# Differential attention with the transposed weights as the stationary operand, and 72-wide transposes of the maxima

## The chip, the cores and the metric

The program runs on one core of a Trainium2 chip. The metric is the time of one execution on the device in microseconds (us). Engines are named as in the profile: PE is TensorE (the matmuls; PEld its loads of the stationary operand), DVE VectorE, ACT ScalarE, POOL GpSimd, SP the engine that issues most DMAs.

## The reference

Two layers of a transformer-like block over 128 context rows and 512 latent rows of width 1024. Each layer projects the rows, runs three groups of heads beside each other, projects back and ends in a gated MLP. The change lies in the two attention groups. Shortened:

```python
def gqa_attend(q, k, v):            # 8 heads of 64, 2 key/value heads
    s = einsum('bqkgd,bskd->bkgqs', q, k) * 64 ** -0.5
    p = softmax(s, axis=-1)
    return einsum('bkgqs,bskd->bqkgd', p, v)

def diff_attend(q, k, v, lam):      # 4 heads, two softmaxes of 32-wide keys each
    s = einsum('bqhcd,bshcd->bhcqs', q, k) * 32 ** -0.5
    p = softmax(s, axis=-1)
    a = p[:, :, 0] - lam * p[:, :, 1]
    return einsum('bhqs,bshd->bqhd', a, v)     # v is 64 wide

o_d = rms_norm(diff_attend(...), diff_subln_g) * (1 - lam_init)
```

Latent rows attend to 512 latent and 128 context keys (640), context rows to the 128 context keys alone.

## The kernel before

Everything is float32; products that need the accuracy of float32 are split into high and low float32r parts, and some are plain float32 matmuls. Rows come in five tiles of 128 (t = 0 the context, 1 to 4 latent). In the attention stage of a layer (`attend`, line 1545, called for tiles 1, 2, 3, 4, 0, numbered i) one tile does the following.

- GQA half: `scores` with queries as stationary operand into PSUM pairs `p`; `maxima` on VectorE; `split_m` (1596) puts a group's four negated maxima and their low parts in an [128, 8] tile `mm`; `m_trans` (1604) turns it by a matmul with the identity, 8 wide, into partitions 64 to 72 of a bank, from where it goes to rows 64 to 72 of `qTm`. Those rows meet rows 64 to 72 of `KL`, which are ones, so that the second score matmul (`c_mm`, keys stationary, 512 columns) comes out with the maximum subtracted. `c_exp` takes the exponential on ScalarE into the weight buffers `whi` and `wlo` (PT slots), `d_mm` (1656) multiplies the values `VG` (64 wide, stationary) with it: two matmuls of 512 columns, one for each half of the array's columns, for each of five key blocks. They gather in bank b3, which `o_read` copies out.
- Row sums: for i < 3 `sum_mm` (1690) multiplies 32 ones with the summed exponentials into 64 rows, `sum_c` copies them, `sum_t` (1701) transposes them in four pieces, `sum_r` takes the reciprocal. For i = 3 and 4 eight matmuls of one column (1675) do it.
- Differential half: scores, exponentials `P` with their row sums, the two softmaxes joined, then for each key block four transposes of `P` (`trans`), a copy to a PT slot, and `d_mm` (1794): four matmuls with `VD` (64 wide) as stationary and 128 columns of transposed weights, in pairs in the two halves of the array's columns. They also gather in bank b3 (`od_b`). `o_read2` (1806) copies it, `n_trans` (1816) turns it back with two transposes, `n_copy` and `n_sq` (1823, 1827) read that bank, and the norm, a last turn and a copy into `mix` follow.
- Keys, in the stage before: `split3` (1302) makes high and low parts of the keys, `k_trans` (1315) transposes them, the GQA keys' low part 64 wide.

Two schedulers set the order. `Schedule` (573) orders the tasks of a layer's attention by priority and by free banks (b3 alone for both halves' results, b0 to b2 for the rest). Then `Graph` (181) plans the whole program fifteen times with durations from `cost` (501), each time with new due times, and emits the order with the shortest planned total; it may split what one task emitted. Each engine then runs its instructions in that order. A float32 matmul's planned duration depends on its stationary width (64 wide: half) and its columns.

## Time and profile before

| | us |
|---|---|
| median of three runs (1703.84 to 1709.37) | 1704.2 |
| the profiled execution | 1706.38 |
| its span, first to last instruction | 1704.3 |
| PE busy | 1674.7 (98%) |
| DVE busy | 1027.5 (60%) |
| ACT busy | 680.7 (40%) |
| POOL busy | 215.0 (13%) |
| granted clock of PE, mean | 0.997 of full speed |

The busy times are unions: matmuls overlap, since one starts to stream while the one before still drains, and the profile models their ends. So the cost of a matmul is read from its start to the start of the next. The names in the rows are those of tiles: `b`, `c` and `p` are PSUM banks, "b<-wlo,VG 128*64 128x512" is a matmul with the stationary operand VG of 128 by 64 and the moving operand wlo with 512 columns. "x4" merges four records that follow each other. One matmul in plain float32 leaves two records.

### The profile page before, as it was taken

To read this page: it belongs to the slowest core of one execution; us is meant where nothing else is said; L and a number is where in the kernel's file an instruction comes from. 1 tells how busy PE (TensorE), PEld (TensorE's weight loads), DVE (VectorE), ACT (ScalarE), POOL (GpSimd) and SP (SyncE) were. 2 spreads that over 40 slices of the span, in tenths; PEclk is the share of its full clock that TensorE was granted. 3 is DMA by queue.
4 is the path that set the end of the run, shared out by engine and by line. 5 is a ranking of instruction groups with operands and counts; after the bars stand their busy time and mean duration, and the time that the engine had idled before them with its cause. 6 is when DMAs were issued, how large, how long until landed. Compare 5 with 4: busy or idle time off the path is not lost.

```text
span 1704.3 us, 24487 instructions
## 1 busy us (share of the span) xinstructions
PE 1674.7 (98%) x9771; PEld 1411.9 (83%) x9771; DVE 1027.5 (60%) x1691; ACT 680.7 (40%) x1268; POOL 215.0 (13%) x308
## 2 busy tenths in 40 slices
PE   7999999999999999999999999999999999999998
PEld 4678766678999879999778896657799998999986
DVE  4757677547665768687446568785666543444423
ACT  6453577536322112232255527774633321223310
POOL 1321234201000000000032112351100000000000
PEclk9999999999999999999999999999999999999999
DMA  9543100253333544454334211003233322222221
GB/s 329 176 147 112 37 13 13 64 172 93 112 110 98 179 142 144 134 169 135 101 127 115 69 50 41 22 3 109 74 99 111 109 85 80 83 73 72 75 70 76
DMA packets 156542, 171.53 MB, mean 101 GB/s; under 512 B 6556, under 2 KB 121612, under 8 KB 155916
## 3 DMA queue, kind: packets, MB, share of 16 engines
q1 hardware_dynamic: 150940, 152.18, 29.0%
q0 software_dynamic: 5488, 17.79, 3.2%
q8 instruction: 77, 1.26, 0.3%
q14 instruction: 37, 0.30, 0.1%
HBM read 163.88 MB, written 6.06 MB: 100 GB/s over the span
## 4 chain that ended last, share of the span: by engine, by line
PE 92%; DVE 3%; ACT 3%; DMA 1%; issue 1%; POOL 0%; ACTq 0%; DVEq 0%; POOLq 0%
PE c L316 48%; PE b L316 41%; PE p L316 3%; DVE xq L316 1%; DVE sq L316 1%; ACT whi L316 1%; ACT xn L316 1%; DVE wlo L316 1%; ACT fu L316 0%; DMA raw<-in_w_mod_dram 0%; ACT junk L316 0%; DVE qsg L316 0%; DVE nmax L316 0%; DVE macc L316 0%; ACT hh L316 0%
## 5 line engine op out<-in xcount | busy, mean ns | idle before, releaser
L316 DVE TENSOR_TENSOR wlo<-raw,whi 128x1024 fp32r<-128x1024 f32 (+1 forms) x188 | 227.3, 1209 | 331.3 <-ACT whi L316 331.0
L316 PE MATMUL c<-hl,whi 128*128 128x322 f32 x1280 | 397.9, 311 | 1.1 <-DVE hl L316 1.1
L316 PE MATMUL c<-hh,whi 128*128 128x322 f32 x1280 | 398.5, 312 | 0.0
L316 ACT ACTIVATE whi<-raw 128x1024 fp32r<-128x1024 f32 (+1 forms) x188 | 195.3, 1041 | 506.9 <-PE b L316 283.6
L316 PE MATMUL c<-hh,wlo 128*128 128x322 f32 x1280 | 397.3, 311 | 0.0
L316 PEld LDWEIGHTS c<-hh,whi 128*128 128x128 f32 x1280 | 241.5, 189 | 2.6 <-issue 2.1
L316 PEld LDWEIGHTS c<-hl,whi 128*128 128x128 f32 x1280 | 241.2, 188 | 1.4 <-DVE hl L316 1.3
L316 PEld LDWEIGHTS c<-hh,wlo 128*128 128x128 f32 x1280 | 241.3, 189 | 0.0
L316 DVE SCALAR_TENSOR_TENSOR macc<-raw,slc,macc 128x1024 f32<-128x1024 f32 x98 | 123.8, 1279 | 16.6 <-DMA raw<-in_w_mod_dram 16.2
L316 DVE TENSOR_REDUCE nmax<-p 128x1 f32<-128x640 f32 x128 | 103.7, 819 | 34.3 <-PE p L316 33.8
L316 PE MATMUL b<-wlo,fh 128*128 128x512 f32 x264 | 104.3, 395 | 0.0
L316 PE MATMUL b<-whi,fh 128*128 128x512 f32 x264 | 104.2, 395 | 0.0
L316 PE MATMUL b<-whi,fl 128*128 128x512 f32 x264 | 104.1, 394 | 0.0
L316 PE MATMUL b<-hh,wlo 128*128 128x322 f32 x320 | 99.7, 311 | 0.0
L316 PE MATMUL b<-hh,whi 128*128 128x322 f32 x320 | 99.5, 311 | 0.0
L316 PE MATMUL b<-hl,whi 128*128 128x322 f32 x320 | 99.5, 311 | 0.0
L316 ACT ACTIVATE tv<-tv 128x644 f32<-128x644 f32 x44 | 32.6, 742 | 140.3 <-DVE tv L316 140.2
L316 DVE SCALAR_TENSOR_TENSOR tv<-asb,vec,tv 128x643 f32<-128x643 f32 x88 | 78.0, 887 | 2.3
L316 DVE TENSOR_TENSOR tv<-tv,c 128x322 f32<-128x322 f32 x88 | 42.5, 488 | 53.1 <-ACT tv L316 27.5
L316 PE MATMUL c<-whi,fh 128*128 128x512 f32 x176 | 69.6, 397 | 0.6 <-DVE tv L316 0.6
L316 PE MATMUL c<-wlo,fh 128*128 128x512 f32 x176 | 69.5, 395 | 0.0
L316 PE MATMUL c<-whi,fl 128*128 128x512 f32 x176 | 69.3, 394 | 0.0
(318 smaller groups left out, 3129.5 us busy)
## 6 DMA issues: line engine op xcount, KB each, us to landing
raw<-in_w_mod_dram SPq DMA_DIRECT2D x96, 512.0 KB, 4.0
raw<-in_ffn_up_dram SPq DMA_DIRECT2D x88, 512.0 KB, 4.7
raw<-in_ffn_down_dram SPq DMA_DIRECT2D x40, 512.0 KB, 3.7
raw<-in_w_in_dram SPq DMA_DIRECT2D x28, 512.0 KB, 4.8
raw<-in_w_in_dram SPq DMA_DIRECT2D x16, 256.0 KB, 5.1
raw<-in_w_out_dram SPq DMA_DIRECT2D x8, 512.0 KB, 3.5
raw<-in_w_out_dram SPq DMA_DIRECT2D x16, 256.0 KB, 3.9
gate<-gd POOLq DMA_DIRECT2D x4, 1024.0 KB, 6.0
```

The costliest lines, as they stand in the source:

```text
L316: getattr(real, name)(*a, **k)
```

## The change

- `d_mm` of the differential half swaps its operands: the transposed weights (128 wide) are stationary, 64 columns of `VD` move, and the output has queries on the partitions. The four heads lie side by side in b3. `o_read2` and `n_trans` go; `n_copy` and `n_sq` read `od_b` itself, so b3 is held until both are done.
- `mm` is one of four fixed tiles of [128, 72] whose first 64 columns are cleared by GpSimd at the start of the stage; `m_trans` is 72 wide and writes partitions 0 to 72. What follows reads 64 to 72 as before.
- The low part of the GQA keys is put first in its stack, and its transpose is 72 wide, of which 64 rows are used.
- `sum_mm` multiplies 64 ones instead of 32, the copy and the transposes are 128 by 128.
- `cost` plans a plain float32 matmul with a stationary operand over 64 wide at 4/2400 us for each column or 0.112 us, whichever is more. Since planned durations and tasks change, so does the order.

```diff
+        if m > 64:
+            return max(4 * n / 2400, 0.112), 0.0
...
-            tt(s[:, :, lo_, :], z, f32(s)[:, :, 0, :], ALU.subtract)
+            tt(s[:, :, lo_, :], z, f32(s)[:, :, hi.start, :], ALU.subtract)
...
-                kst["g", t] = split3(T(prj, [128, 2, 3, 64], "kstg", F32R, bufs=1), zv("kg", t), 2, 64, slice(0, 2))
+                kst["g", t] = split3(T(prj, [128, 2, 3, 64], "kstg", F32R, bufs=1), zv("kg", t), 2, 64, slice(1, 3))
...
-                    PE.transpose(pv[:, u, :], v[:, u, 0:128], ident)
-                    PE.transpose(pv[0:64, 2 + u, :], v[:, u, 128:192], ident)
+                    PE.transpose(pv[:, u, :], v[:, u, 64:192], ident)
+                    PE.transpose(pv[0:72, 2 + u, :], v[:, u, 0:72], ident)
...
+        mx_tiles = [T(at, [128, 72], f"mm{x}") for x in range(4)]
+        for x in mx_tiles:
+            G.memset(x[:, 0:64], 0.0)
...
-                def split_m(mm=mm, nm_=nm_):
-                    mm["t"] = T(SM, [128, 8], "mm", bufs=6)
-                    V.tensor_copy(mm["t"][:, 0:4].bitcast(F32R), nm_["t"])
-                    tt(mm["t"][:, 4:8], nm_["t"], mm["t"][:, 0:4], ALU.subtract)
+                def split_m(mm=mm, nm_=nm_, x=mx_tiles[(2 * i + a_) % len(mx_tiles)]):
+                    mm["t"] = x
+                    V.tensor_copy(x[:, 64:68].bitcast(F32R), nm_["t"])
+                    tt(x[:, 68:72], nm_["t"], x[:, 64:68], ALU.subtract)
...
-                    PE.matmul(bk.t[64:72, 0:128], mm["t"], ident, start=True, stop=True)
+                    PE.matmul(bk.t[0:72, 0:128], mm["t"], ident, start=True, stop=True)
...
-                        PE.matmul(sb.t[32 * a_:32 * a_ + 32, :], ones[:, 0:32], x[a_].t, start=True, stop=True)
+                        PE.matmul(sb.t[64 * a_:64 * a_ + 64, :], ones[:, 0:64], x[a_].t, start=True, stop=True)
...
-                        PE.transpose(sb2.t[:, 64 * u:64 * u + 64], box["s"][:, 128 * u:128 * u + 128], ident[0:64, 0:64])
+                        PE.transpose(sb2.t[:, 128 * u:128 * u + 128], box["s"][:, 128 * u:128 * u + 128], ident)
...
-            od_b = Buf(o_bank, 1)
+            od_b = Buf(o_bank, 2)
...
-                    for x in range(2):
-                        for a_ in range(2):
-                            h = 2 * x + a_
-                            PE.matmul(od_b.t[64 * a_:64 * a_ + 64, 128 * x:128 * x + 128], VD[:, v, 64 * h:64 * h + 64],
-                                      pt.t[:, 128 * h:128 * h + 128], start=k == 0 and x == 0, stop=k == len(vs) - 1 and x == 1)
+                    for h in range(4):
+                        PE.matmul(od_b.t[:, 64 * h:64 * h + 64], pt.t[:, 128 * h:128 * h + 128], VD[:, v, 64 * h:64 * h + 64],
+                                  start=k == 0 and h == 0, stop=k == len(vs) - 1 and h == 3)
...
-            def o_read2():
-                oc2.t = T(at, [128, 512], oc2.tag)
-                act(oc2.t[:, 0:256], od_b.t[:, 0:256])
...
-                two(tb.t, oc2.t)
...
-                act(od.t, heads(tb.t[:, 0:256], 64))
+                act(od.t, heads(od_b.t[:, 0:256], 64))
...
-                act(bx["sq"], heads(tb.t[:, 0:256], 64), AF.Square)
+                act(bx["sq"], heads(od_b.t[:, 0:256], 64), AF.Square)
```

How the order moves, at three places of the first layer. The numbers behind a name tell one tile from the next of the same name, `ident` is the identity of a transpose, `qsd` and `qsg` are query stacks. The first place is on PE in the GQA half of the second tile, where value products (VG) stand among scores. Before the change PE has there:

```order
L316 MATMUL p_503_2544<-KL_814,qTm_437_2274 128x320
L316 MATMUL b_483_2485<-whi_2158,VG_842 64x512
L316 MATMUL b_504_2554<-qTg_310_2018,KG_1259 128x512
L316 MATMUL b_504_2554<-qTm_311_854,KL_814 128x512
L316 MATMUL b_506_2563<-ident_109,qsd_2291 96x128 x4
L316 MATMUL b_483_2485<-whi_2158,VG_842 64x512
L316 MATMUL p_509_2571<-KG_1259,qTg_436_2276 128x320
```

Two value products stand there, each alone between full-width matmuls. After the change, at the same place on PE:

```order
L316 MATMUL p_508_2579<-KL_807,qTm_439_2223 128x320
L316 MATMUL b_509_2585<-ident_109,qsd_2306 96x128 x4
L316 MATMUL b_491_2515<-whi_2127,VG_839 64x512
L316 MATMUL b_491_2515<-wlo_2181,VG_839 64x512
L316 MATMUL b_511_2597<-qTg_310_2022,KG_1259 128x512
```

Two value products that stood alone, with scores and transposes between them, stand side by side. In the same tile three stand in a row, twice.

The second place is on PE where the differential half of that tile starts its value products: sums, `mm` and `VD`. Before the change:

```order
L316 MATMUL b_533_2691<-whi_2102,VD_867 64x128 x3
L316 MATMUL b_534_2697<-ident_109,sums_2687 128x64 x4
L316 MATMUL b_533_2691<-whi_2102,VD_867 64x128
L316 MATMUL b_536_2705<-ident_109,P_466_2417 128x128
L316 MATMUL b_536_2705<-ident_109,P_474_2451 128x128
L316 MATMUL b_536_2705<-ident_109,P_484_2487 128x128
L316 MATMUL b_536_2705<-ident_109,P_502_2531 128x128
L316 MATMUL p_539_2718<-KD_939,qTd_429_2246 128x320 x2
L316 MATMUL b_541_2721<-ident_109,mm_2707 8x128
L316 MATMUL b_533_2691<-whi_2102,VD_867 64x128 x2
L316 MATMUL b_542_2730<-ident_109,rx_2716 128x128 x4
L316 MATMUL b_533_2691<-whi_2102,VD_867 64x128 x2
```

The first `d_mm` is cut in two by the sums' transposes (three matmuls and one), the second by the spread of the reciprocals (`rx`), with `mm` beside it. After the change, on PE from the sums' transposes on:

```order
L316 MATMUL b_530_2693<-ident_109,sums_2683 128x128 x4
L316 MATMUL b_532_2701<-VD_865,whi_2107 128x64 x4
L316 MATMUL b_533_2706<-ident_109,P_466_2422 128x128
L316 MATMUL b_533_2706<-ident_109,P_474_2456 128x128
L316 MATMUL b_533_2706<-ident_109,P_484_2492 128x128
L316 MATMUL b_533_2706<-ident_109,P_499_2530 128x128
L316 MATMUL p_536_2717<-KD_946,qTd_431_2259 128x320 x2
L316 MATMUL b_537_2720<-ident_109,mm_368_2030 72x128
L316 MATMUL b_532_2701<-VD_865,wlo_2113 128x64
L316 MATMUL b_538_2726<-ident_109,rx_2713 128x128 x4
L316 MATMUL b_532_2701<-VD_865,wlo_2113 128x64 x3
```

The first `d_mm` is in one piece now; the second is still cut by `rx`, and `mm` still stands beside a part of it, with 128 and 72 columns of the array instead of 64 and 8.

The third place is on ACT at the end of the first tile's differential half: the reads of its result. Before the change:

```order
L316 ACTIVATE ob_479_2467<-b_452_2353 128x256
L316 ACTIVATE wlo_2107<-b_475_2463 128x512
L316 ACTIVATE P_482_2478,sum_2418<-p_472_2454,nmax_2393 128x640
L316 ACTIVATE P_484_2487,sum_2418<-p_476_2469,nmax_2475 128x640
L316 ACTIVATE osq_2497<-b_487_2491 128x256
L316 ACTIVATE whi_2102<-b_477_2473 128x512
L316 ACTIVATE od_489_2509<-b_487_2491 128x256
```

The copy `ob` alone reads the bank of the value products there (b_452); `osq` and `od` read another bank, after the turn. After the change, on ACT from the first read on:

```order
L316 ACTIVATE od_479_2479<-b_453_2357 128x256
L316 ACTIVATE P_482_2486,sum_2423<-p_472_2458,nmax_2388 128x640
L316 ACTIVATE P_484_2492,sum_2423<-p_476_2472,nmax_2477 128x640
L316 ACTIVATE whi_2107<-b_477_2475 128x512
L316 ACTIVATE osq_2505<-b_453_2357 128x256
```

The copy `ob` is gone, `od` and `osq` read the bank of the value products itself (b_453), and two exponentials and a copy stand between them; that bank is b3, which the next tile's GQA half needs.

## Rows read from the trace of the kernel before

**Rows 1.** The page, chain that ended last: its time by engine, whole span.

```profile
PE 92%; DVE 3%; ACT 3%; DMA 1%; issue 1%; POOL 0%; ACTq 0%; DVEq 0%; POOLq 0%
```

**Rows 2.** Busy us of each engine (instructions), clock, DMA: the two attention stages.

```profile
196.00:345.00 149.00, 148.36 (x832) 90.69 (x831) 107.23 (x197) 102.36 (x232) 54.39 (x62) 0.98 0.14 42
1036.00:1183.00 147.00, 146.39 (x830) 92.14 (x831) 110.25 (x198) 103.55 (x233) 54.95 (x62) 1.00 0.12 40
```

**Rows 3.** TensorE's instructions in time: start us, us, what; full-width neighbours.

```profile
209.15 0.40 PE L316 MATMUL b<-qTg,KG 128*128 128x512 f32 x1
209.38 0.39 PE L316 MATMUL b<-qTm,KL 72*128 72x512 f32 x1
```

**Rows 4.** The same view: transposes, then the one-column sums.

```profile
309.48 0.66 PE L316 MATMUL b<-ident,P 128*128 128x128 f32 x4
309.97 1.84 PE L316 MATMUL b<-ones,acc 128*128 128x1 f32 x16
311.67 0.63 PE L316 MATMUL b<-ident,P 128*128 128x128 f32 x4
```

**Rows 5.** The same view: a whole d_mm, and a half one.

```profile
228.24 0.40 PE L316 MATMUL b<-qTm,KL 72*128 72x512 f32 x1
228.56 0.66 PE L316 MATMUL b<-whi,VD 128*64 128x128 f32 x8
229.15 0.50 PE L316 MATMUL b<-qTg,KG 128*128 128x512 f32 x1
229.49 0.39 PE L316 MATMUL b<-qTm,KL 72*128 72x512 f32 x1
...
318.63 0.44 PE L316 MATMUL b<-wlo,VD 128*64 128x128 f32 x4
319.00 0.66 PE L316 MATMUL b<-KD,qTd 96*128 96x128 f32 x4
```

**Rows 6.** The same view: a pair of VG, and a single one.

```profile
207.13 1.08 PE L316 MATMUL b<-whi,VG 128*64 128x512 f32 x4
208.14 0.42 PE L316 MATMUL p<-KD,qTd 96*128 96x320 f32 x1
...
214.82 0.31 PE L316 MATMUL p<-KG,qTg 128*128 128x320 f32 x1
214.97 0.31 PE L316 MATMUL p<-KL,qTm 72*128 72x320 f32 x1
215.21 1.07 PE L316 MATMUL b<-wlo,VG 128*64 128x512 f32 x2
216.22 0.42 PE L316 MATMUL p<-KG,qTg 128*128 128x320 f32 x1
```

**Rows 7.** The same view: transposed maxima, and the transposes of the sums.

```profile
218.71 0.31 PE L316 MATMUL p<-KG,qTg 128*128 128x320 f32 x1
218.95 0.39 PE L316 MATMUL b<-ident,mm 128*8 128x128 f32 x2
219.26 0.42 PE L316 MATMUL p<-KL,qTm 72*128 72x320 f32 x1
...
223.16 0.46 PE L316 MATMUL b<-ident,sums 64*128 64x64 f32 x4
223.55 0.56 PE L316 MATMUL p<-KD,xq 96*128 96x320 f32 x2
```

**Rows 8.** Weight loads by shape: count, busy us, mean ns of one, idle.

```profile
L316 PEld LDWEIGHTS b<-ones,acc 128*128 128x128 f32 x32 | 3.7, 192 | 0.0
```

**Rows 9.** ScalarE by shape: exponentials, copy of 512 columns, squares of 256.

```profile
L316 ACT ACTIVATE P<-p,nmax 128x640 f32<-128x640 f32 x64 | 50.8, 796 | 9.4 <-DVE nmax L316 8.1
...
L316 ACT ACTIVATE ob<-b 128x512 f32<-128x512 f32 x10 | 5.9, 593 | 4.9 <-PE b L316 4.8
...
L316 ACT ACTIVATE osq<-b 128x256 f32<-128x256 f32 x10 | 3.8, 382 | 2.8 <-PE b L316 2.8
```

**Rows 10.** As rows 2: the stretch in which the clock fell.

```profile
321.30:328.20 6.90, 6.90 (x18) 3.04 (x17) 1.93 (x10) 2.51 (x8) 1.82 (x5) 0.51 0.31 77
```

More of the change, by code (lines that the diff above doesn't have):

```diff
@@ L1692, in sum_mm @@
                     for a_ in range(2):
-                        PE.matmul(sb.t[32 * a_:32 * a_ + 32, :], ones[:, 0:32], x[a_].t, start=True, stop=True)
+                        PE.matmul(sb.t[64 * a_:64 * a_ + 64, :], ones[:, 0:64], x[a_].t, start=True, stop=True)
                 s1 = sc.add([("PE", 0.5, sum_mm)], aT, p_, takes=[sb], reads=accs)
                 def sum_c(e, sb=sb, box=box):
-                    box["s"] = T(at, [64, 512], "sums")
-                    act(box["s"], sb.t[0:64]) if e is S else e.tensor_copy(box["s"], sb.t[0:64])
+                    box["s"] = T(at, [128, 512], "sums")
+                    act(box["s"], sb.t) if e is S else e.tensor_copy(box["s"], sb.t)
                 s1 = sc.add([("S", 0.48, lambda f=sum_c: f(S)), ("V", 0.6, lambda f=sum_c: f(V))], [s1], p_, reads=[sb])
@@ L1796, in d_mm @@
                         od_b.t = bank(od_b.tag)
-                    for x in range(2):
-                        for a_ in range(2):
-                            h = 2 * x + a_
-                            PE.matmul(od_b.t[64 * a_:64 * a_ + 64, 128 * x:128 * x + 128], VD[:, v, 64 * h:64 * h + 64],
-                                      pt.t[:, 128 * h:128 * h + 128], start=k == 0 and x == 0, stop=k == len(vs) - 1 and x == 1)
+                    for h in range(4):
+                        PE.matmul(od_b.t[:, 64 * h:64 * h + 64], pt.t[:, 128 * h:128 * h + 128], VD[:, v, 64 * h:64 * h + 64],
+                                  start=k == 0 and h == 0, stop=k == len(vs) - 1 and h == 3)
                 d_prev = sc.add([("PE", 0.48, d_mm)], [e_, d_prev], p_ + 2, takes=[od_b] if k == 0 else [], reads=[pt])
             p_ = base + P_TD + I_T * (3 + len(vs))
-            oc2 = Buf(s_ob, 1)
-            def o_read2():
-                oc2.t = T(at, [128, 512], oc2.tag)
-                act(oc2.t[:, 0:256], od_b.t[:, 0:256])
-            n1 = sc.add([("S", 0.27, o_read2)], [d_prev], p_, takes=[oc2], reads=[od_b])
-            tb = Buf(banks, 2)
             def two(dst, src):
@@ L1814, in two @@
                     PE.transpose(dst[:, 128 * x:128 * x + 128], src[:, 128 * x:128 * x + 128], ident)
-            def n_trans():
-                tb.t = bank(tb.tag)
-                two(tb.t, oc2.t)
-            n2_ = sc.add([("PE", 0.22, n_trans)], [n1], p_, takes=[tb], reads=[oc2])
             od = Buf(s_od, 1)
@@ L1824, in n_copy @@
                 od.t = T(at, [128, 4, 64], od.tag)
-                act(od.t, heads(tb.t[:, 0:256], 64))
+                act(od.t, heads(od_b.t[:, 0:256], 64))
             def n_sq():
                 bx["sq"] = T(at, [128, 4, 64], "osq")
-                act(bx["sq"], heads(tb.t[:, 0:256], 64), AF.Square)
-            n3 = sc.add([("S", 0.27, n_copy)], [n2_], p_, takes=[od], reads=[tb])
-            n4 = sc.add([("S", 0.27, n_sq)], [n2_, n3], p_, reads=[tb])
+                act(bx["sq"], heads(od_b.t[:, 0:256], 64), AF.Square)
+            n3 = sc.add([("S", 0.27, n_copy)], [d_prev], p_, takes=[od], reads=[od_b])
+            n4 = sc.add([("S", 0.27, n_sq)], [d_prev, n3], p_, reads=[od_b])
             def n_sum():
```

2 lines of the change are left out of this document (1 added, 1 removed).

## The prediction, made before the result was known

> **What bounds the kernel now.** I read the chain that ended last first, then the busy time of the two attention stages, then TensorE's instructions one by one. The chain runs over TensorE for 92% of the span [rows 1]. The two attention stages last 149 and 147 us; TensorE is busy for all but 0.6 us of each, VectorE for 107 and 110 us, ScalarE for 102 and 104 [rows 2]. So in the stages that the change touches nothing but TensorE's own instruction stream sets the time, and the question is what each of its instructions costs there. A "busy" TensorE is not one that streams, so I price by the distance from one start to the next, not by the printed durations (they overlap).
>
> **The plain prices.** Beside other full-width matmuls one of 320 columns takes 0.15 us to the next start and one of 512 columns 0.23 [rows 3, 6]. Four transposes right behind a narrow piece take 0.49, so at most 0.12 each with the way out of that piece in it; I take 0.11. Eight one-column matmuls show as 16 records, so a plain float32 matmul leaves two; the 16 take 1.70, 0.106 each [rows 4].
>
> **What a narrow matmul costs.** I call narrow what uses 64 or fewer columns or rows of the array. Take one d_mm of the differential half: the 512-column matmul ahead of it lasts 0.32 to the next start instead of 0.23, its eight records take 0.59, and the 512-column matmul behind it lasts 0.34 instead of 0.23 [rows 5]. So each trip into the narrow form and out again puts some 0.09 and 0.11, together 0.20, on its full-width neighbours, and one d_mm is worth 0.79. Broken into two halves, as the order often has it, a half takes 0.37 itself and the like of 0.10 at either side: 0.57 [rows 5]. Two pairs more make 0.22, so a pair streams in 0.11, and 0.59 less four pairs leaves 0.15 inside for filling and emptying. A value product of the GQA half (VG) takes 0.24 - 0.15 ahead, 1.01 itself, some 0.10 behind: 1.20. Two of them side by side also take 1.01 [rows 6], so the second is free if the order leaves it beside the first. The transposed maxima (mm, 8 wide) cost 0.09 + 0.31 and some 0.10 behind, 0.50; the four transposes of the row sums (64 by 64) take 0.39 themselves, 0.58 with both sides [rows 7].
>
> **The change part by part, both layers together.** Counts are from the program's order.
>
> *VG* itself is unchanged but stands otherwise: before in 61 pieces (38 single, 23 pairs), after in 48 (24 single, 14 pairs, 8 threes, 2 fours). Before 61 x 1.20 = 73.2. After 38 x 1.20 + 10 x 2.06 = 66.2; the 2.06 is a piece with a second pair, 0.86 more, which is 1.01 less the 0.15 for filling and emptying. Gain 7.0.
>
> *The differential d_mm*, 42 of them. Before: 42 x 0.79 = 33.2, and since they stand in 54 pieces, 12 times a second half at 2 x 0.57 - 0.79 = 0.35, 4.2 more: 37.4. After: the transposed weights are the stationary side, 128 wide, and 64 value columns stream. No row of before shows a float32 matmul of that shape. Nearest is the one-column matmul with the same stationary width, 0.106 a record [rows 4]; 128-column transposes at 0.11 lie on the other side of 64 columns, so I take 0.11: 42 x 8 x 0.11 = 37.0. The bounds are 0.05 (half the 0.11 that a 128-column pair took) and 0.19, the mean duration of a weight load of that width, if no load were hidden [rows 8]. Gain 0.4, between 20 and -26.
>
> The Trainium skill speaks against this swap: "TensorEngine Tiling (Array Packing)", Performance Considerations, wants a matmul with a small streamed side turned so that the small side is stationary and two run side by side in column tiles. That is the form of before; what the swap costs by this rule alone is rival 4. The same page, Key Properties, says that a change of tiling mode drains TensorE; the 0.20 at d_mm's neighbours and the 0.15 inside agree with that and, 42 x 0.35 = 14.7 and the 4.2 of broken pieces, weigh as much as the doubled streaming.
>
> *Maxima 72 wide*: 20 x 0.50 = 10.0 before; after two full-width records of 128 columns, 20 x 0.22 = 4.4. Gain 5.6. *Sums*: 6 groups of four transposes, 6 x 0.58 = 3.5 before, 24 x 0.11 = 2.6 after. Gain 0.9. The sum matmuls keep two pieces side by side and their 512 columns: nothing. ScalarE's copy of the sums has the same 512 columns in a row: nothing.
>
> *Shared borders*: 26 of before's narrow pieces touch another narrow one (mm beside VD, sums inside VD), so 26 x 0.20 = 5.2 of the prices above were never paid. Loss 5.2.
>
> *The removed turn* (o_read2, n_trans): 20 transposes on TensorE, 20 x 0.11 = 2.2 gained, and ten ScalarE copies of 0.38 (the shape of osq [rows 9]), hidden before as well.
>
> *The new hold on bank b3*: n_copy and n_sq now read od_b itself, and the next tile's first VG needs that bank. In tiles 1 and 2 of both layers ScalarE does od, two exponentials and an eviction before osq: about 0.38 + 2 x 0.80 + 0.59 + 0.38 = 2.95 [rows 9]. TensorE has 6 x 0.15 + 8 x 0.23 = 2.7 of other work meanwhile. A wait of 0.25 four times, 1.0 lost; between 0 and 4 x 1.
>
> *Keys' low rows 72 wide* and the halves of the key split in another order: the same number of transposes; a transpose keeps its 128 streamed columns and its 0.11. Nothing. *Eight small memsets* on GpSimd, before the first maxima: GpSimd is busy for 54 of 149 us [rows 2]. Nothing. *The planner's new prices* move instructions in the first 25 us and in the attention; elsewhere the order is the same but for names.
>
> **Sum.** -7.0 - 0.4 - 5.6 - 0.9 + 5.2 - 2.2 + 1.0 = -9.9. The profiled execution took 1706.4 us (its span 1704.3 and 2.1 around it), 2.2 above the median of 1704.2. So 1696.5 for such an execution, and 1694.3 against the median; the start, ordered anew, may give or take 1. I say 1694.5.
>
> **The rivals.**
> 1. *The freed time turns into waits.* With TensorE 5 us shorter per layer, maxima on VectorE or exponentials on ScalarE end last in places, bank b3 above all. For: ScalarE and VectorE are busy for some 70% of these stages [rows 2]. Against: TensorE waited next to nothing there. If half is lost: 1699.5.
> 2. *The clock.* At the end of the first layer's attention the granted clock was 0.51 over 6.9 us, that is TensorE mostly at 1.2 instead of 2.4 GHz, after one-column matmuls, transposes and VD; in the second layer the same stretch ran at 1.00 [rows 2, 10]. After the change this stretch streams no more than before: eight transposes, the one-column matmuls and VD at 64 columns stand there together. If both layers fall, or an earlier place does, each time costs about 3 us (half of 6.9): 1697.5 to 1700.5. If the present one goes, 3 less: 1691.5.
> 3. *Slower: the loads of the new stationary side show.* Each of the 336 records brings 128 columns of weights in and streams only 64. If loads were not hidden, a record would last 0.19, not 0.11: 336 x 0.08 = 27 more, 1721. It turns to a loss where a record lasts over 0.11 + 9.9/336 = 0.14. Against it: the one-column records have loads of 0.19 as well and still follow each other at 0.106 [rows 4, 8].
> 4. *Slower: pairs side by side are what counts.* If d_mm's neighbours stay as slow as they are and its 0.15 inside stays too, for whatever reason, only the streaming changes, from four pairs to eight records: 42 x (0.88 - 0.44) = 18.5 lost instead of 0.4 gained, 1713. Against it: a 512-column matmul without a narrow neighbour takes 0.23, every time one of them has it 0.32 to 0.34 [rows 3, 5]. This is where the Trainium skill's rule on small streamed sides, named above, would end.
> 5. *More than that*: the shorter chain at the end of each attention (one ScalarE copy, one pair of transposes) or a clock that stays up: 1690.
>
> **How the numbers follow.** The forecast has 0.68, its own range 1690 to 1699. Rival 1 has 0.13, rival 2 0.09, rival 3 0.04, rival 4 0.02, rival 5 0.04. About 0.3%, 5.1 us, is what a measurement of this kernel can tell from no change. Range 1689 to 1702. Faster by more than 0.3% (under 1699.1) is the forecast, rival 5 and a part of rival 2: 0.75. Within 0.3%: rival 1, the rest of 2, some of the forecast: 0.19. Slower: rivals 3 and 4: 0.06.
>
> **What would show it.** In the profile after: d_mm's eight records 0.88 from the first start to the next, and a 0.23 behind and ahead of them, not 0.32 and 0.34; mm 0.22; sums 0.44; VG pieces at 1.2 and 2.1, fewer of them; both attention stages some 4 to 5 us shorter with TensorE still busy throughout; no idle TensorE ahead of the first VG of a tile, or 0.25. Wrong would be records at 0.15 or more, TensorE waiting for osq by 1 us, or stages as long as before with waits in them. The rest of the program should take the same time.

## The result, and the profile after

The kernel after the change takes 1722.4 us (median of 5 runs, 1719.2 to 1728.8), the kernel before beside it 1707.4 (1703.8 to 1710.7): a ratio of 1.0095, 95% interval 1.0065 to 1.0124. That is 15 us slower where 10 us less were forecast. The runs of after had a mean granted clock of 0.985 to 0.991 (median 0.989), those of before 0.993 to 0.999 over the whole record (median 0.997). The medians and ratios here and below leave out three runs, one each of before, e6 and e11, that took at least a fifth longer than all others.

The profiled execution of after, the slowest of its five, took 1728.8 us, 22.4 more than that of before. By landmarks on TensorE (the first GQA score, then the first matmul with `mah`, which ends the attention stage), the start took 3.4 us more, the first attention stage 11.7, the second 7.1, and all the rest 0.2. The windows of [rows 2] lie some 10 us later than these landmarks. The two stages in whole, by the view of busy time by window (window, length, then busy us and instructions of PE, PEld, DVE, ACT, POOL, then the granted clock), first of before:

```profile
185.70:338.10 152.40, 151.32 (x866) 93.98 (x864) 111.27 (x206) 106.29 (x243) 54.20 (x62) 0.98 0.10 29
1025.40:1173.10 147.70, 146.11 (x852) 92.50 (x850) 112.25 (x207) 107.58 (x244) 55.06 (x63) 1.00 0.09 29
```

and of after:

```profile
189.10:353.20 164.10, 157.84 (x857) 112.59 (x856) 114.14 (x208) 103.29 (x236) 56.15 (x68) 0.92 0.08 24
1040.70:1195.50 154.80, 147.82 (x840) 103.97 (x838) 113.93 (x208) 104.40 (x237) 55.63 (x67) 0.97 0.08 27
```

Length less PE busy is the time in which TensorE had nothing to do: 1.1 and 1.6 us before, 6.3 and 7.0 after. And the clock fell, from 0.98 and 1.00 to 0.92 and 0.97: 37.5 us of the two stages ran at half clock (0.50, which is 1.2 GHz) instead of 6.8, and about half of such time is lost (sixteen records of VD take 3.3 us in it, eight 0.81 outside). So the 18.8 us that the stages lost in this execution are 10.6 of idle time and 15.3 of clock, while the rest, what TensorE's own work takes at full clock, became 7.1 shorter. The chain that ended last, which ran over VectorE for 3% [rows 1], now does so for 7%:

```profile
PE 89%; DVE 7%; ACT 2%; POOL 1%; DMA 1%; issue 1%; SPq 0%; POOLq 0%; ACTq 0%; DVEq 0%
```

TensorE's waits in the first stage of after (what waits, for what: us in total, times, longest); before, none of them was longer than 0.4 us:

```profile
PE p L316 <- ACT P L316: 2.4, 3, 2.0
PE b L316 <- DVE od L316: 1.3, 1, 1.3
PE b L316 <- ACT qTm L316: 0.9, 2, 0.6
PE p L316 <- DVE nmax L316: 0.8, 3, 0.3
PE b L316 <- DVE mm L316: 0.8, 1, 0.8
```

The prices, on the other hand, are those forecast. One d_mm of after, from TensorE's instructions in time (start us, us, what), beside [rows 5]:

```profile
263.18 0.40 PE L316 MATMUL b<-qTm,KL 72*128 72x512 f32 x1
263.41 1.00 PE L316 MATMUL b<-VD,whi 128*128 128x64 f32 x8
264.22 0.47 PE L316 MATMUL b<-qTg,KG 128*128 128x512 f32 x1
264.54 0.39 PE L316 MATMUL b<-qTm,KL 72*128 72x512 f32 x1
```

0.23 to the first record, 0.81 for the eight, 0.32 for the matmul behind them: 0.90 with what the neighbours lose, 0.88 forecast.

Where the waits are made is seen on VectorE. In the middle of the first stage (after; VectorE's and GpSimd's instructions in time, then TensorE's; the bracket is the idle time ahead and what ended it):

```profile
266.00 0.88 DVE L316 SCALAR_TENSOR_TENSOR P<-P,ra,P 128x640 f32<-128x640 f32 x1
...
267.95 0.22 DVE L316 SCALAR_TENSOR_TENSOR ra<-ra,nl,sum 128x1 f32<-128x1 f32 x1
...
272.73 1.79 DVE L316 SCALAR_TENSOR_TENSOR P<-P,ra,P 128x640 f32<-128x640 f32 x1
274.44 1.51 DVE L316 TENSOR_TENSOR od<-od,ors 128x256 f32<-128x256 f32 x1
...
275.99 1.37 DVE L316 TENSOR_TENSOR od<-od,sg 128x256 f32<-128x256 f32 x1
277.29 0.81 DVE L316 TENSOR_REDUCE nmax<-p 128x1 f32<-128x640 f32 x1
...
272.57 3.10 POOL L316 TENSOR_TENSOR acc<-acc,wlo 128x512 f32<-128x512 f32 x2
275.63 4.08 POOL L316 TENSOR_TENSOR acc<-acc,whi 128x512 f32<-128x512 f32 x3
...
275.84 0.31 PE L316 MATMUL p<-KL,qTm 72*128 72x320 f32 x1
277.42 0.44 PE L316 MATMUL b<-ident,od 128*128 128x128 f32 x2 [1.26 <-DVE od L316]
278.15 0.41 PE L316 MATMUL p<-KG,qTg 128*128 128x320 f32 x1 [0.29 <-DVE nmax L316]
```

While GpSimd adds up exponentials (`acc`, five adds in a row), VectorE's P<-P,ra,P takes 1.79 instead of 0.88, and the two steps of the norm 1.51 and 1.37 instead of 0.42; the reduction nmax, which reads PSUM, keeps its 0.81. TensorE stands for 1.26 us until `od` is there, and again for the maximum that queued behind it. Some 28 us later the same is seen, ahead of the longest wait of the stage:

```profile
300.87 1.66 DVE L316 SCALAR_TENSOR_TENSOR P<-P,ra,P 128x640 f32<-128x640 f32 x1
...
302.64 1.27 DVE L316 SCALAR_TENSOR_TENSOR ra<-ra,nl,sum 128x1 f32<-128x1 f32 x1
303.95 1.85 DVE L316 SCALAR_TENSOR_TENSOR P<-P,ra,P 128x640 f32<-128x640 f32 x1
...
300.57 1.28 POOL L316 TENSOR_TENSOR acc<-whi,wlo 128x512 f32<-128x512 f32 x1 [14.53 <-ACT wlo L316]
302.61 1.29 POOL L316 TENSOR_TENSOR acc<-whi 128x512 f32<-128x512 f32 x1 [0.76 <-ACT whi L316]
303.86 1.26 POOL L316 TENSOR_TENSOR acc<-acc,wlo 128x512 f32<-128x512 f32 x1
...
307.51 0.56 PE L316 MATMUL p<-KD,xq 96*128 96x320 f32 x2 [1.96 <-ACT P L316]
```

The one-column step ra<-ra,nl,sum takes 1.27 instead of 0.22. The exponential of P for which TensorE waits had itself waited 2.5 us for a maximum that stood behind these three. The stretches of both stages at half clock (windows as above):

```profile
278.80:282.20 3.40, 3.40 (x11) 1.36 (x10) 2.02 (x3) 0.59 (x1) 0.92 (x1) 0.50 0.00 0
309.60:313.00 3.40, 3.40 (x5) 0.79 (x4) 3.40 (x9) 1.48 (x3) 1.92 (x2) 0.51 0.00 0
323.20:343.70 20.50, 20.50 (x86) 17.90 (x84) 6.48 (x21) 8.11 (x25) 1.89 (x5) 0.50 0.01 2
1057.10:1063.90 6.80, 6.60 (x10) 2.30 (x11) 3.16 (x7) 3.76 (x10) 1.25 (x1) 0.50 0.28 99
1162.90:1166.30 3.40, 3.40 (x5) 0.79 (x4) 3.40 (x9) 1.48 (x3) 1.97 (x2) 0.50 0.00 0
```

The first two begin 1.4 and 2.1 us after the end of the two waits shown, and the last in the same way after a wait of 1.97 us in the second stage; the fourth stands among waits of 0.6 to 0.7 us. One wait of 1.26 us in the second stage has no fall behind it. The long stretch, 20.5 us, has no wait ahead of it: transposes, one-column matmuls, `mm` and VD stand there, and TensorE is busy throughout. Before, the clock fell for 6.9 us at the end of the first stage [rows 10] and not in the second.

The collisions are not new. Groups of VectorE's instructions by shape over both stages (count, busy us, mean ns of one), before:

```profile
L316 DVE TENSOR_TENSOR od<-od,ors 128x256 f32<-128x256 f32 x10 | 7.9, 793 | 3.8 <-POOL ors L316 3.6
L316 DVE TENSOR_TENSOR od<-od,sg 128x256 f32<-128x256 f32 x10 | 5.3, 534 | 0.1
```

and after:

```profile
L316 DVE TENSOR_REDUCE nmax<-p 128x1 f32<-128x640 f32 x128 | 103.2, 817 | 43.0 <-PE p L316 42.7
...
L316 DVE TENSOR_TENSOR od<-od,ors 128x256 f32<-128x256 f32 x10 | 9.5, 947 | 2.9 <-POOL ors L316 2.8
L316 DVE TENSOR_TENSOR od<-od,sg 128x256 f32<-128x256 f32 x10 | 9.0, 902 | 0.1
```

They got worse for `od`, but a good part of them was there before. What is new is that TensorE waits for them. The Trainium skill describes such a collision ("SBUF — State Buffer", Who interferes with whom): a VectorE instruction with two inputs in SBUF contends with a GpSimd instruction that reads SBUF, and a reduction never contends. The rows above agree, with 0.42 against 1.37 to 1.51 and an unchanged 0.82.

### The profile page after: what moved, and what is told of

It is laid out like the page before. It is cut to its first block, busy times and chain, and to the rows that moved or that the text cites. A ratio compares the mean times of both kernels' runs of the same rounds, so it can differ in the third digit from the quotient of the medians.

```text
span 1727.0 us, 24436 instructions
## 1 busy us (share of the span) xinstructions
PE 1687.1 (98%) x9751; PEld 1446.4 (84%) x9751; DVE 1033.3 (60%) x1693; ACT 675.1 (39%) x1254; POOL 221.1 (13%) x318
## 3 DMA queue, kind: packets, MB, share of 16 engines
q8 instruction: 77, 1.26, 0.3%
## 4 chain that ended last, share of the span: by engine, by line
PE 89%; DVE 7%; ACT 2%; POOL 1%; DMA 1%; issue 1%; SPq 0%; POOLq 0%; ACTq 0%; DVEq 0%
PE c L316 48%; PE b L316 38%; PE p L316 2%; DVE nmax L316 2%; DVE wlo L316 1%; DVE P L316 1%; DVE xq L316 1%; DVE od L316 1%; DMA raw<-in_w_mod_dram 1%; ACT whi L316 0%; DVE sq L316 0%; ACT fu L316 0%; POOL acc L316 0%; ACT xn L316 0%; DVE qsg L316 0%
## 5 line engine op out<-in xcount | busy, mean ns | idle before, releaser
L316 DVE SCALAR_TENSOR_TENSOR macc<-raw,slc,macc 128x1024 f32<-128x1024 f32 x98 | 123.9, 1279 | 13.2 <-DMA raw<-in_w_mod_dram 12.8
```

Of the source, the lines that this page charges most:

```text
L316: getattr(real, name)(*a, **k)
```

## The experiments

Three theories stood against each other at first. **A**: the clock falls because the swapped d_mm streams 64 columns. **B**: the order is at fault, planned with prices that are too low, so that others come late. **E**, after the first four runs: the order lays VectorE's collisions with GpSimd on TensorE's path. All runs in one table; idle is a stage's length less its PE busy, the clock that of the stage, and the last column the part of the stage in which the trace has the clock at 0.50, each from the profiled execution, first stage and second. Length less idle time less half of the last column is called the stream: what TensorE's own work takes at full clock. Both stages together it is 294.0 us before and 286.9 after.

| | median us | ratio to before, 95% | stages us | idle us | clock | at half clock, us |
|---|---|---|---|---|---|---|
| before | 1707.4 | | 152.4, 147.7 | 1.1, 1.6 | 0.98, 1.00 | 6.8, 0.0 |
| after | 1722.4 | 1.0065 to 1.0124 | 164.1, 154.8 | 6.3, 7.0 | 0.92, 0.97 | 27.3, 10.2 |
| e1 | 1717.6 | 1.0037 to 1.0081 | 155.2, 155.7 | 6.3, 7.0 | 0.98, 0.97 | 6.8, 10.2 |
| e2 | 1708.2 | 1.0001 to 1.0032 | 151.2, 149.0 | 3.0, 3.4 | 0.98, 0.99 | 6.8, 3.4 |
| e3 | 1698.6 | 0.9934 to 0.9972 | 145.3, 143.7 | 2.5, 1.7 | 0.98, 0.98 | 6.8, 6.8 |
| e4 | 1725.1 | 1.0088 to 1.0143 | 160.6, 157.1 | 5.5, 6.7 | 0.95, 0.97 | 17.1, 10.2 |
| e5 | 1697.1 | 0.9930 to 0.9955 | 144.2, 145.3 | 2.0, 2.6 | 0.98, 0.98 | 6.8, 6.8 |
| e6 | 1709.6 | 1.0000 to 1.0028 | 154.1, 149.6 | 8.1, 7.4 | 0.94, 0.97 | 17.1, 10.2 |
| e7 | 1702.4 | 0.9965 to 0.9990 | 155.1, 144.3 | 1.8, 2.9 | 0.93, 1.00 | 20.5, 0.0 |
| e8 | 1702.4 | 0.9964 to 0.9985 | 150.1, 148.6 | 1.3, 1.7 | 0.98, 0.99 | 6.8, 3.4 |
| e9 | 1707.3 | 0.9988 to 1.0010 | 154.0, 149.2 | 1.0, 1.6 | 0.97, 0.99 | 10.2, 3.4 |
| e10 | 1701.0 | 0.9960 to 0.9991 | 154.1, 143.7 | 1.1, 1.8 | 0.93, 1.00 | 20.5, 0.0 |
| e11 | 1692.9 | 0.9905 to 0.9931 | 143.4, 142.5 | 1.1, 1.8 | 0.98, 0.99 | 6.8, 3.4 |
| e12 | 1700.4 | 0.9956 to 0.9982 | 146.3, 145.0 | 1.8, 2.8 | 1.00, 1.00 | 0.0, 0.0 |
| e13 | 1702.3 | 0.9954 to 0.9976 | 148.8, 146.0 | 1.8, 2.8 | 0.98, 0.99 | 6.8, 3.4 |
| e14 | 1703.2 | 0.9966 to 0.9991 | 148.3, 148.4 | 1.5, 2.1 | 0.99, 0.99 | 3.4, 3.4 |

**e1, VD streamed 128 wide, same order.**

```diff
-PE.matmul(od_b.t[:, 64 * h:64 * h + 64], pt.t[:, 128 * h:128 * h + 128], VD[:, v, 64 * h:64 * h + 64],
+PE.matmul(od_b.t[:, 128 * h:128 * h + 128], pt.t[:, 128 * h:128 * h + 128], VD[:, v, 128 * (h // 2):128 * (h // 2) + 128],
...
```

> The kernel after the change, with the same order of instructions on every engine, but each of d_mm's 336 differential records streams 128 columns of VD instead of 64 (half of the product is not used). In the profile after, TensorE stood at half clock in ten stretches of together some 51 us (before: three, some 14 us with the tail), and TensorE waited some 7 us more in each attention stage. Theory A (the clock: 64-column streaming beside transposes and one-column matmuls is too little work, and the half-clock stretches come from it): the half-clock stretches in the two attention stages, 37 us together, shrink to under 10 us; the time falls by 8 to 18 us, to 1705 to 1714. Theory B (waits: the new order lets VectorE and ScalarE be late, and the clock falls because TensorE waits): records stay at 0.11 us, the same waits stand at the same places, half-clock stretches stay about as long; 1718 to 1726, as after.

1717.6 us, 4.8 less than after. The windows of its stages:

```profile
188.40:343.60 155.20, 148.88 (x857) 105.58 (x856) 114.15 (x208) 103.45 (x236) 56.19 (x68) 0.98 0.09 25
1030.70:1186.40 155.70, 148.69 (x840) 104.93 (x838) 114.15 (x208) 104.84 (x237) 56.07 (x67) 0.97 0.08 27
```

The idle times are those of after to a tenth of a us, since the order is the same. The clock of the first stage is back at 0.98 and the stage 8.9 us shorter; the second has 0.97 as in after, and nothing changed. Half clock in both stages falls from 37.5 to 17.0 us, not to under 10, and the time misses the ranges of both theories. The clocks of all runs speak for A, too (0.991 to 0.997, against 0.985 to 0.991 in after). So A accounts for the long stretch of the profiled execution and at most for about a third of the loss; the intervals of the two ratios overlap. The larger part is elsewhere.

**e2, the planner's price put right.**

```diff
-            return max(4 * n / 2400, 0.112), 0.0
+            return 0.224, 0.0
```

> The kernel after the change, with the planner's price of a plain float32 matmul with over 64 stationary columns set to what the trace of after shows, 0.224 us (two records of 0.111), instead of 0.112 to 0.213. Nothing but the order changes. Theory A (the clock falls because of what TensorE streams): 1714 to 1726, with half-clock stretches of 30 us or more. Theory B (the planner thought TensorE 84 x 2 x 0.11 = 18 us shorter than it is in the differential products, so its order lets the others be late where it plans them in time): the waits of TensorE in the attention stages go from about 14 us each back to 7, half-clock stretches with them, and the time falls by 14 to 24 us, to 1698 to 1708.

1708.2 us, 14.2 less, with half the idle time and a clock of 0.98 and 0.99, VD still 64 wide. B is right that the order decides, and that the clock largely follows the waits. But the level of before is only reached, not passed. VectorE's steps are no faster here than in after:

```profile
L316 DVE TENSOR_TENSOR od<-od,ors 128x256 f32<-128x256 f32 x10 | 9.4, 941 | 4.2 <-POOL ors L316 4.1
L316 DVE TENSOR_TENSOR od<-od,sg 128x256 f32<-128x256 f32 x10 | 9.1, 906 | 0.1
```

Yet TensorE's waits in the first stage no longer have one for `od`.

**e3, everything but the swap.** d_mm, `o_read2` and `n_trans` of the differential half as before, the rest as after.

```diff
-                    for h in range(4):
-                        PE.matmul(od_b.t[:, 64 * h:64 * h + 64], pt.t[:, 128 * h:128 * h + 128], VD[:, v, 64 * h:64 * h + 64],
+                    for x in range(2):
+                        for a_ in range(2):
+                            h = 2 * x + a_
+                            PE.matmul(od_b.t[64 * a_:64 * a_ + 64, 128 * x:128 * x + 128], VD[:, v, 64 * h:64 * h + 64],
...
+            n1 = sc.add([("S", 0.27, o_read2)], [d_prev], p_, takes=[oc2], reads=[od_b])
...
+            n2_ = sc.add([("PE", 0.22, n_trans)], [n1], p_, takes=[tb], reads=[oc2])
...
```

> The kernel after the change without the swap of the differential products (VD stationary, 128 columns of weights streamed in pairs, with the copy and the turn back, as before); maxima and keys 72 wide, sums by 64 ones and the planner's new price stay. By the prediction's own sum: maxima 5.6 less and sums 0.9 less, some shared borders back: 1702 to 1705 against 1707.4 of the kernel before. Theory A (the swap's 64-column streaming brings the clock down): half-clock stretches no longer than 17 us, 1700 to 1707. Theory B (order by wrong prices): here the wrong price touches only the maxima (planned 0.21, right) and the one-column matmuls (planned half of what they take), so 1702 to 1712, with waits between those of before and of after.

1698.6 us: 8.8 less than before, more than the 6.5 of maxima and sums, in part because 34 of its 50 VG pieces are pairs side by side (before, 23 of 61). At the forecast's 1.20 a piece that alone is 13.2 us of TensorE's work; the stream is 16.0 shorter than that of before, and more idle time and lower clock take part of it back.

**e4, the swap alone.** The kernel before with the swap and the new price (the block of e3 the other way round, and the two lines of `cost`).

```diff
+        if m > 64:
+            return max(4 * n / 2400, 0.112), 0.0
```

> The kernel before with the swap of the differential products and the planner's new price alone; maxima 8 wide, keys 64 wide, sums by 32 ones as before. Theory A (the swap brings the clock down): half-clock stretches of 30 us or more and 1718 to 1730. Theory B (order by prices that halve the swapped products): 1712 to 1726, with waits of 12 us or more in each attention stage. If neither the swap nor its price is at fault: 1703 to 1708, since by the prediction's sum the swap alone gains some 2 to 4 us.

1725.1 us, 17.7 more than before. The whole loss, and more, comes with the swap and its price; TensorE waits 3.6 us for `od` in the first stage alone.

**e5, without the swap, right price**: e3 with the line of e2.

```diff
-            return max(4 * n / 2400, 0.112), 0.0
+            return 0.224, 0.0
```

> The kernel after the change without the swap of the differential products, as in the run without the swap (1698.6 us, 0.995 of before), but planned with the price 0.224 us that a plain float32 matmul with over 64 stationary columns shows in the traces (there: 0.213 for the maxima, 0.112 for a one-column matmul). With the swap this price gave 14 us (1722.4 to 1708.2). Theory B1 (it is the price of the 336 swapped records that led the planner astray, TensorE planned 18 us too short): little is left to gain here, 1696 to 1701. Theory B2 (any small change of prices throws the order about, by chance): anywhere from 1690 to 1708. If it falls under 1696, the one-column price mattered too.

1697.1 us, 0.58% less than before: the best of all that leave nothing out. The price is worth 1.6 here, against 14.2 with the swap. That speaks for B1: the 336 swapped records, planned at half their time, were what mattered.

**e6, bank b3 free one instruction earlier**, on e2.

```diff
-            od_b = Buf(o_bank, 2)
+            od_b = Buf(o_bank, 1)
...
-                act(bx["sq"], heads(od_b.t[:, 0:256], 64), AF.Square)
+                act(bx["sq"], od.t, AF.Square)
...
-            n4 = sc.add([("S", 0.27, n_sq)], [d_prev, n3], p_, reads=[od_b])
+            n4 = sc.add([("S", 0.27, n_sq)], [n3], p_)
```

> The swap with the right price (1708.2 us), but the square is taken from the copy od instead of bank b3, so that b3 is free after one ScalarE instruction as in the kernel before, not after two. In the run with the right price TensorE waited some 21.5 us in the two attention stages (before: 13; without the swap: 15.5), and 24 value products stood alone (without the swap: 16). Theory C (the longer hold on b3 is what pushes the value products apart and makes the waits): 1699 to 1704, with 16 to 20 single VG pieces. Theory D (the hold costs nothing; the waits come from VectorE, which is late with the norm and the maxima): 1705 to 1711, with the same waits.

1709.6 us, as the run before it, but by another way, which neither theory gave. C is right on the pieces: the longer hold does push the value products apart, for here 36 of 45 VG pieces are pairs and only 8 single (e2: 24 of 48 single), and the stream is 274.6 us, the shortest of all runs and 14.1 less than in e2. It is wrong on the waits, and so is D: they more than double, to 8.1 and 7.4 us idle (the longest, 2.5 us, for a maximum), and with 27.3 us at half clock instead of 10.2 all of the gain is lost again. What this order would take without VectorE's slow steps was not tried.

**e7, GpSimd's adds cut, order of after.** The later adds work on 24 columns, the first of each group stays 512 wide; the row sums are incomplete.

```diff
-                            e.tensor_tensor(out=new.t, in0=x.t, in1=y.t, op=ALU.add)
+                            w_ = 24 if e is G and new is x else 512
+                            e.tensor_tensor(out=new.t[:, 0:w_], in0=x.t[:, 0:w_] if new is x else ones[:, 0:1].to_broadcast([128, 512]), in1=y.t[:, 0:w_], op=ALU.add)
...
```

> The kernel after the change with the same order on TensorE, VectorE and ScalarE, but GpSimd's adds of the exponentials (20 or 21 a layer, some 1.38 us each) work on 24 columns instead of 512, and the first add of a group takes a constant for one of its inputs: the row sums are left incomplete. Theory E (VectorE is late because its instructions take two to three times as long while GpSimd adds: od<-od,sg 0.90 us instead of 0.42, P<-P,ra,P up to 1.86 instead of 0.88; 12 us in each attention stage): VectorE's busy time in each stage falls by 6 to 10 us, the wait of 1.4 us for od and those for the maxima go, the attention stages get 3 to 7 us shorter each, and the time is 1708 to 1716 instead of 1722.4. Theory F (VectorE's slow stretches lie off the path): 1719 to 1725.

1702.4 us: 20.0 less than after, more than either theory gave. VectorE is busy for 104 us a stage instead of 114, the idle time is 1.8 and 2.9, the second stage took 144.3. The first still has 0.93, from a stretch of 20.5 us like that of after. Of the 19.5 us that the two stages gained, 8.6 are idle time and 8.5 clock: the short falls behind the waits are gone with the waits.

**e8, before with the new price alone.** It reaches only the one-column matmuls.

```diff
+        if m > 64:
+            return max(4 * n / 2400, 0.112), 0.0
```

> The kernel before with nothing but the planner's new price, which here reaches only the one-column matmuls (planned 0.112 us instead of 0.214; they take 0.22). It shows what a changed price does to the order alone. Theory B1 (a price that is too low for few instructions does little): 1706 to 1710. Theory B2 (orders differ by chance by many us): anywhere from 1700 to 1716.

1702.4 us, 5.0 less than before, where B1 expected no more than 1.4: a new order alone is worth 0.3% here, by chance. This is one draw and no bound, but a difference of this size between two orders proves nothing of what stands in them. What the price does with the swap lies beyond it: the two orders with the low price took 1722.4 and 1725.1 us (after, e4), the two with the right one 1708.2 and 1709.6 (e2, e6).

**e9, GpSimd's adds cut in the kernel before**: the edit of e7.

```diff
+                            w_ = 24 if e is G and new is x else 512
```

> The kernel before, same order, with GpSimd's adds of the exponentials cut to 24 columns and a constant in place of one input of the first add (row sums left incomplete), as it was done to the kernel after, which then fell by 20 us, from 1722.4 to 1702.4. Theory E (the kernel after lost because its order lays the slowed VectorE instructions on the path, that of before does not): before gains little, 0 to 7 us: 1700 to 1707. Theory G (GpSimd's adds tax every order alike, and the loss of after has another cause): before gains 15 to 22 us: 1685 to 1692.

1707.3 us, ratio 0.9999. VectorE's busy time falls by 9 us a stage here too (111 and 112 to 103), and nothing comes of it. Together with e7 this decides: before carries collisions of the same kind off the path, after on it. G falls.

**e10 and e11, the same cut with the right price, with and without the swap**: the edit of e7 on e2 and on e5.

```diff
+                            w_ = 24 if e is G and new is x else 512
```

> The swap planned with the right price (1708.2 us), same order, with GpSimd's adds of the exponentials cut to 24 columns (row sums left incomplete). By the prediction's sum, which had no such collisions in it, the swap and the rest are worth about 10 us against the kernel before. Theory E: the waits that the right price left, some 8 us above those of before, go too: 1694 to 1701. If they have another cause: 1703 to 1709.

> Without the swap, planned with the right price (1697.1 us), same order, GpSimd's adds cut to 24 columns (row sums left incomplete). TensorE waited some 2 us more in its attention stages than in those of before. Theory E: 1690 to 1696, and so the swap, with the collisions taken away on either side, costs or gives less than 6 us. Theory G: 1677 to 1684.

1701.0 us, the upper end of E's range, and 1692.9, within it. e10 is where e7 is, so with most of the collisions gone the price is worth only 1.4; it had mattered by where the collisions fell. Between e10 and e11 stand 8.1 us, more than the 6 that E allowed for the swap. In the profiled executions the first stage differs by 10.7, the second by 1.2 (143.7 against 142.5), but e10 has 20.5 us at half clock in the first and e11 6.8 there and 3.4 in the second. By the stream e11 is 6.7 us shorter; at the forecast's prices 5.0 of these are VG, which stands in 51 pieces of 1.20 there, against 38 of 1.20 and 10 of 2.06.

**e12, both causes taken away, order of after**: the edits of e1 and e7.

```diff
+                            w_ = 24 if e is G and new is x else 512
...
+PE.matmul(od_b.t[:, 128 * h:128 * h + 128], pt.t[:, 128 * h:128 * h + 128], VD[:, v, 128 * (h // 2):128 * (h // 2) + 128],
```

> The kernel after, same order, with both suspected causes removed: VD streamed 128 columns wide (half of the product not used) and GpSimd's adds cut to 24 columns (row sums left incomplete). With VD alone it took 1717.6 us, with the adds alone 1702.4, and the latter's profile still has 20 us of half clock in the first attention stage. If waits and clock are all that went wrong: 1694 to 1699, as predicted for the change; the half clock in both attention stages under 7 us. If the half clock comes from something else: 1700 to 1705.

1700.4 us. Its stages run at full clock:

```profile
188.60:334.90 146.30, 144.50 (x857) 104.15 (x855) 103.96 (x208) 103.42 (x236) 32.05 (x68) 1.00 0.09 27
1021.80:1166.80 145.00, 142.18 (x840) 103.42 (x838) 103.65 (x207) 104.61 (x237) 31.28 (x67) 1.00 0.09 28
```

Together they are 8.8 us shorter than those of before. The time still misses the 1694 to 1699, and not by half clock in the stages: in the profiled execution the start is 2.9 us longer than in before. It need not be a property of the order, since e9, in the order of before, starts 2.1 later than before itself. The 2.0 us between e12 and e7 lie within the spread of their runs (1699.5 to 1703.9 and 1698.1 to 1708.1).

**e13, GpSimd as busy, but off the memory, order of after.** The later adds are powers on 6 columns; the row sums are not computed.

```diff
+                            s_ = e is G and new is x
+                            w_ = 6 if s_ else 512
+                            e.tensor_tensor(out=new.t[:, 0:w_], in0=x.t[:, 0:w_] if new is x else ones[:, 0:1].to_broadcast([128, 512]), in1=y.t[:, 0:w_], op=ALU.pow if s_ else ALU.add)
...
```

> The kernel after, same order on TensorE, VectorE and ScalarE, with GpSimd's later adds of the exponentials replaced by a power on 6 columns (row sums not computed): by the row of ors<-oss,mhalf, 1.03 us for 4 columns, it should hold GpSimd about as long as an add does (1.3 to 1.6 us), but it reads and writes next to nothing. Cutting the adds to 24 columns had brought 20 us (1722.4 to 1702.4), and that run both spared VectorE the collision and let GpSimd be done earlier. Theory E (it is the collision that slows VectorE): as with the cut adds, 1699 to 1706, VectorE busy some 103 us a stage. Rival H (GpSimd itself was late, and buffers and sums came free too late): 1717 to 1725, as after.

1702.3 us. The view of after's first place, VectorE and then GpSimd:

```profile
270.66 0.42 DVE L316 TENSOR_TENSOR od<-od,ors 128x256 f32<-128x256 f32 x1
...
271.11 0.42 DVE L316 TENSOR_TENSOR od<-od,sg 128x256 f32<-128x256 f32 x1
...
269.67 2.62 POOL L316 TENSOR_TENSOR acc<-acc,wlo 128x6 f32<-128x6 f32 x2
272.25 3.90 POOL L316 TENSOR_TENSOR acc<-acc,whi 128x6 f32<-128x6 f32 x3
```

and the groups of VectorE over both stages:

```profile
L316 DVE TENSOR_REDUCE nmax<-p 128x1 f32<-128x640 f32 x128 | 103.9, 820 | 47.2 <-PE p L316 47.1
...
L316 DVE TENSOR_TENSOR od<-od,sg 128x256 f32<-128x256 f32 x10 | 4.2, 423 | 0.1
L316 DVE TENSOR_TENSOR od<-od,ors 128x256 f32<-128x256 f32 x10 | 4.2, 421 | 2.9 <-POOL ors L316 2.8
```

GpSimd is busy for 54.6 and 53.8 us a stage, against 56.2 and 55.6 in after, and stands beside the same steps of the norm; these take 0.42. Where the first adds of a group still are 512 wide, P<-P,ra,P still takes up to 1.68. H falls: not GpSimd's own lateness, but what its adds do to VectorE.

**e14, all adds on VectorE, on e5**, nothing left out.

```diff
-[("G", 1.23, lambda f=addup: f(G)), ("V", 0.6, lambda f=addup: f(V))]
+[("V", 0.6, lambda f=addup: f(V))]
```

> Without the swap, right price (1697.1 us), with all adds of the exponentials given to VectorE (0.6 us each as planned, against 1.4 on GpSimd), nothing left out; the order is planned anew. Under theory E VectorE gains some 8 us a stage from the end of the collisions and pays some 12 for the 20 adds. If the collisions' waits were what is left: 1692 to 1696; if VectorE's longer queue makes waits of its own: 1697 to 1706.

1703.2 us, 6.1 more than e5 with no more idle time: the order is another again, and a difference of this size is that of e8. It gives no answer on the collisions; it is no better version.

## Why the prediction was wrong, point by point

*The prices of the sum* held. d_mm took 0.90 (0.88 forecast, against 0.79 before), though not by the parts that were forecast: the eight records took 0.81, not 0.88, and the matmul behind them 0.32, not 0.23. VG pieces that stand alone or side by side took 1.20, those with a second pair 2.05, the transposed maxima 0.22 to 0.24. The bounds on the new shape, 0.05 to 0.19 a record, were settled at 0.10 to 0.11, which rules out rivals 3 and 4. The sum without its wait for bank b3 was 10.9 us less. In the order of after, with most collisions gone and 64 columns as in the change, the stream is 9.6 us (e7) and 8.9 us (e13) shorter than before, so the sum was some 1 to 2 us too good; 0.8 of that are d_mm's 0.02, the rest was not traced to a term.

*"In the stages that the change touches nothing but TensorE's own instruction stream sets the time"* is the step that failed. It was true of the order of before [rows 2], and the prediction carried it over to an order that the planner made anew. It said of the new prices only that they "move instructions", and put that at no cost. In the new order TensorE had nothing to do for 13.3 us of the two stages instead of 2.7, and stood at half clock for 37.5 us instead of 6.8; its own sign of being wrong, stages as long as before with waits in them, came true. By the planner TensorE needs 0.112 us for a swapped matmul, by the trace 0.22; 168 of them make some 18 us that the plan believes TensorE does not need. With the price put right alone (e2), 14.2 of the 15 us are back. That the differential products stand in the plan where VectorE is in time, and run where it isn't, is a reading of this; the planned times were not laid beside the trace.

*Rival 1* had the mechanism (maxima on VectorE and exponentials on ScalarE end last) and a size four times too small: half of 10 us lost, where e7 and e13 show 20. It named bank b3 as the first place; in e6 a shorter hold on it left more waits, not fewer. What it lacked was GpSimd. The one sentence on it, "GpSimd is busy for 54 of 149 us", counts its load and not what it does to its neighbour, though the trace of before showed it: od<-od,ors 793 ns on average and od<-od,sg 534, for two steps of one shape that take 420 undisturbed.

*Rival 2*, the clock, had the mechanism and the place, the end of the first layer's attention. It was put at 3 us a fall; e1 against after shows 8.9 us in that stage, 4.8 in the median. The clock as a whole cost more than the idle time: between the median clocks of before and after lie 0.008, which over some 1720 us is an estimated 14 us. Most of it follows the waits: the order of after with the collisions cut ran at 0.992 to 0.997 (e7, e13), with them at 0.985 to 0.991. The two causes overlap: 4.8 and 20.0 apart, 22.0 together.

*The hold on bank b3*, 1.0 us, was not seen as a wait: none for osq is in the list. It acts through the order instead, by where the value products can stand (e6). *The start*, "give or take 1", took 3.4 us more in the profiled execution; by e9, which starts 2.1 later in the order of before, a good part of that can be chance.

What stays open: why the long stretch at half clock comes in one execution and not in the next (e7 and e10 had 20.5 us of it in the first stage, e13, whose 64-column records stand in the order of e7, did not). The two profiles with 128 streamed columns, e1 and e12, lack it, and the runs of e1 had a higher clock than those of after; but those of e12 (0.994 to 0.996) do not stand apart from those of e7 (0.992 to 0.997), so that the 64 columns make it likelier is not shown. Open, too, is what the order of e6, with the shortest stream, would take with GpSimd's adds cut, and what a planner would make that knows of the collisions.

## What to carry to other kernels

When a change alters the prices of a planner, the new order is part of the change. Before saying that a stage is bound by one engine and will stay so, look for instructions of one shape that take twice as long at some places: they show a slack that the present order happens to have and the next may not. Read idle time, clock and the work itself apart: e6 has the least work of all these kernels and is no faster for it. Split a change and time its parts: here everything but the swap gave 0.5% (e3), and the swap, with its price, took 1.4% (after against e3).

## What the runs showed of the hardware

An add of 128x512 on GpSimd slows VectorE's steps with two SBUF inputs from 0.42 to 1.4 us, from 0.88 to 1.8, and one of a single column from 0.22 to 1.27. How long GpSimd is busy does not decide it: a power on 6 columns, 1.3 to 1.4 us long on average, leaves the 0.42 as it is (e13). That the amount of data which GpSimd moves decides fits this, but width and operation were changed together. The Trainium skill ("SBUF — State Buffer", Who interferes with whom) calls the contention an exclusive lock. The adds look like one: od<-od,sg starts 0.36 us into the first of three adds that take 4.08 together, and ends 1.37 later, about as if it had waited for that add and then taken its 0.42. The powers, which read SBUF as well, don't, and here the measurement decides.

A plain float32 matmul with 128 stationary columns costs 0.10 to 0.11 us a record whether 1, 64 or 128 columns stream: 16 records of one column took 1.70 us [rows 4], the eight of a d_mm 0.81 with 64 columns (after) and 0.81 with 128 (e1). The clock that TensorE was granted in the first stage was not the same, 0.92 and 0.98, that of the second was, 0.97 and 0.97.
